# Five more block pairs in seven products, and the SSD output product as filler of attention

## The chip, the cores and the metric

The kernel runs on one core of a Trainium2 chip. The metric is the time of one execution in device microseconds; a kernel is run three times and the median is taken. Besides that, one execution is recorded by the hardware profiler, and all tables of this document come from such records.

## What is computed

One decoder block on 1024 tokens of width 1024, in float32. Two token mixers, a Mamba-2 SSD and a differential attention, run on the same normed input `h`; each is followed by its own output product and a sigmoid gate; the merged result goes through one more product, a residual, and a gated conv-FFN. Cut to what matters here:

```python
h = rms_norm(x, pre_norm1_w) * (1 + sc1) + sh1            # sc, sh, g: six rows of silu(c) @ w_ada + b_ada
z, xbc, dt_raw, q, k, v, gates = split(h @ w_in)
y_ssd = ssd_branch(z, silu(conv(xbc)), dt_raw)            # 8 chunks of 128 tokens, 16 heads in 2 groups
                                                          # ends with * silu(z), RMS over a group, * norm_w
y_att = diff_attention(rope(q), rope(k), v)               # 8 heads, two softmaxes each, 8 query blocks
gate_ssd, gate_att = split(sigmoid(gates))
merged = gate_ssd * (y_ssd @ w_ssd_o) + gate_att * (y_att @ w_attn_o)
x = x + g1 * rms_norm(merged @ w_out, post_norm1_w)
u_gate, u_val = split(conv3(rms_norm(x) @ w_up))
x = x + g2 * rms_norm((gelu(u_gate) * u_val) @ w_down, post_norm2_w)
```

## The kernel before, in words

**Products.** Every float32 product is made of three passes: both operands are split into a high part (`fp32r`, a copy on ScalarE) and a low part (a subtraction on DVE), and TensorE adds high x high, high x low and low x high in one PSUM bank. A *block* is 128 output columns of a weight matrix, over all 1024 tokens. Taken directly it is 2 token halves x 8 k x 3 = 48 matmuls of 128x512. Two blocks can be taken as a *pair*: the 2x2 scheme of Strassen and Winograd, seven products (`order`, L292) of 4 k x 3 matmuls, 84 in all, at the price of sums of weights (`x_sum`, four per pair), sums of `h` made once (`t1` to `t4`), and additions where the banks are emptied.

**Stages, in order of time.** (1) Norm, and the first blocks directly. (2) The *pairs* (loop at L728, list at L293): ten pairs, two of gates of the SSD (`gs`), two `rope` and one `qk` pair (a block of `w_q` with one of `w_k`), five of the SSD's `xbc`. What a pair's result still needs (`post`, L456: tanh and store for gates; RoPE; split and store for q, k; a conv of four taps and SiLU for `xbc`) is worked off during the next pair, step by step, at the products that `steps_at` (L508) names. In the same loop single `ada_sum`s (a dot product of a 128x1024 tile with the condition, on DVE; 32 in all, `ada_load` fetches a tile for each) stand at the products named in `ada_at` (L511). (3) The *z product* (L953): three column thirds of eight token blocks, 24 products `nz`; 20 ada sums; at `nz` 22 `ada_end` (L940): three short DVE operations, a transposition on TensorE, two stores. From `nz` 8 the *down sums* start (`down_sums`, L812): for each of 11 blocks of `w_down`, two loads of 512 KB, four DVE sums of 128x512 and two stores, for the seven products of the down projection. (4) The *SSD chunks* (L1234): 16 units `u` (chunk, group). TensorE's gaps are filled with the v product (`v_stream`, `fill`); three down sums stand in each unit; the normed y of a chunk (`chunk_norm`) is stored to `yd`. (5) A stage of its own (L1307): q block 3, the 64 transpositions of y (`turn_y`, four banks in turn, 16 after another) with the norm weight applied and split, then the SSD output product `so`, eight blocks directly, gated and stored to `msd`. (6) *Attention* (L1623): 64 items (head j, query block i). For each: scores of the next item, transpositions of this item's probabilities, values. The softmax of the next item runs on DVE and ScalarE meanwhile: mask, maximum, two exps, reciprocal, and at L1522 the difference of the two, which the next item's transpositions at L1530 wait for. TensorE's time is filled by `dense_stream` (L1425): 17 blocks, directly: k 3, q and k of 4 to 7, and the eight attention gates `ga`. (7) Attention's output product, `w_out`, and the FFN: the up product in pairs with `up_conv` and `up_gsum` worked off at products (`early`, `convs`), the down product in seven products.

**What sets the order.** TensorE, DVE, ScalarE and SP (in attention GpSimd in SP's place) follow the order of the code within each stage (`manual_schedule`); the planner may interleave the end of one such stage with the start of the next, and it sets the other queues. Every DMA goes through SP's queue but six stores. Work that is to be done "by the way" goes to a list (`later`, `bg`), from which `run_bg(n)` takes the next n pieces; `need(tag)` runs the list until a piece is done. A fill is one k, three matmuls.

In attention an item gets a quota of fills by

```python
share = [5, 4, 4, 4, 5, 5, 5, 4]                                              # by query block i
quota = (j * sum(share) + sum(share[: i + 1])) * nfill // (8 * sum(share)) - done
f1 = quota // 2                       # behind the first transpositions
f2 = (quota - f1 + 1) // 2            # behind the values of the first four key blocks; the rest at the end
```

with `nfill` = 16 per block less `NFIRST` + `NLAST` (L1618).

## Time and profile before

| | |
|---|---|
| three runs | 1846.46, 1847.04, 1847.34 us |
| the profiled execution | 1846.69 us; span from first to last instruction 1844.9 us |
| granted TensorE clock, mean | 0.999 |
| DMA | 327.5 MB, 178 GB/s over the span |
| q 3, turns and `so` (544 to 649 us) | 105 us |

A row of the view by line or by wait gives the line, the engine, the operation, tiles written and read, shapes, the count, the busy time and the mean duration of one; behind the bar the idle time of the engine ahead of these instructions and what ended most of it. A row of the timeline gives start and duration in us from the span's start, and in brackets the idle time before it. Busy time of TensorE includes the overlap of a matmul with the next one, so it is not a measure of how fast matmuls follow each other.

### The profile page before, as it was taken

The numbers are of one execution on the slowest core, as the hardware profiler recorded it, in microseconds if no ns is written. First come the engines' busy times: TensorE is split into PE (matmuls) and PEld (weight loads), VectorE is DVE, ScalarE is ACT, GpSimd is POOL, SyncE is SP. The second block draws the span as 40 slices with busy tenths as digits, with TensorE's granted clock in tenths as the row PEclk, the third lists the DMA queues.
The fourth block names the chain that finished last, engine by engine and source line by source line (L and its number), as shares of the span: only waits on it lengthen the run. The fifth ranks groups of instructions, "written<-read, shape, count | busy, mean of one in ns | idle before, by whom it ended". The sixth has DMA issues, their size and how long they took to land.

```text
span 1844.9 us, 24221 instructions
## 1 busy us (share of the span) xinstructions
PE 1818.2 (99%) x8889; PEld 1518.2 (82%) x8889; DVE 1304.1 (71%) x2000; ACT 877.4 (48%) x1714; POOL 123.5 (7%) x122
## 2 busy tenths in 40 slices
PE   9999999999999999999999999999999999999998
PEld 7788889987788888888887888887878888888886
DVE  7887897778954267677667563588988888876545
ACT  4454453256542145665666232555545454564532
POOL 0000000035630000000000000000000000000001
PEclk9999999999999999999999999999999999999999
DMA  9464546878664746665724663122223222378744
GB/s 373 163 231 157 184 129 220 309 244 301 239 236 140 237 127 172 185 171 156 193 83 165 239 215 141 58 86 109 103 109 112 100 97 109 115 237 306 239 154 158
DMA packets 130726, 327.52 MB, mean 178 GB/s; under 512 B 14208, under 2 KB 38672, under 8 KB 130608
## 3 DMA queue, kind: packets, MB, share of 16 engines
q1 hardware_dynamic: 129648, 322.83, 52.2%
q0 software_dynamic: 960, 3.15, 0.5%
q8 instruction: 70, 1.15, 0.2%
q14 instruction: 48, 0.39, 0.1%
HBM read 228.53 MB, written 95.30 MB: 176 GB/s over the span
## 4 chain that ended last, share of the span: by engine, by line
PE 76%; DVE 12%; ACT 5%; DMA 4%; issue 2%; SPq 0%; POOL 0%; POOLq 0%; DVEq 0%; ACTq 0%
PE upx L1852 3%; PE upx L1851 3%; PE upx L1853 3%; PE o L1543 3%; PE xx L422 2%; PE xx L423 2%; PE xx L424 2%; PE dx L2216 2%; PE dx L2217 2%; PE dx L2215 2%; PE dy L2217 2%; PE dy L2216 2%; PE dy L2215 2%; PE so L119 2%; PE ao L119 2%
## 5 line engine op out<-in xcount | busy, mean ns | idle before, releaser
L1851 PE MATMUL upx<-t,wu_t 128*128 128x512 f32 x264 | 103.3, 391 | 0.3 <-DVE cv L2280 0.2
L1852 PE MATMUL upx<-t,wu_t 128*128 128x512 f32 x264 | 102.9, 390 | 0.2 <-DVE t L1969 0.2
L1853 PE MATMUL upx<-t,wu_t 128*128 128x512 f32 x264 | 102.8, 389 | 0.0
L1825 ACT ACTIVATE wu_t<-sab 128x512 fp32r<-128x512 f32 x57 | 34.1, 627 | 129.7 <-DVE sab L1842 129.7
L1531 ACT COPY aT<-at 128x512 f32<-128x512 f32 (+2 forms) x96 | 46.0, 479 | 94.5 <-PE at L1530 94.5
L1543 PEld LDWEIGHTS o<-vt,aT 128*128 128x128 f32 x576 | 74.8, 191 | 10.3 <-ACT aT L1531 6.3
L96 DVE TENSOR_TENSOR g_lo<-gst,g_hi 128x1024 fp32r<-128x1024 f32 (+1 forms) x42 | 47.5, 1135 | 50.6 <-ACT g_hi L95 50.6
L1543 PE MATMUL o<-vt,aT 128*128 128x128 f32 x576 | 81.2, 277 | 0.6 <-ACT aT L1531 0.3
L95 ACT ACTIVATE g_hi<-gst 128x1024 fp32r<-128x1024 f32 (+1 forms) x42 | 41.4, 988 | 64.8 <-DMA gst<-gld_s 34.8
L1504 DVE TENSOR_REDUCE nmx<-sc 128x1 f32<-128x640 f32 (+3 forms) x64 | 65.6, 1025 | 2.2
L1484 PE MATMUL sc<-kst,qst 128*128 128x512 f32 (+2 forms) x192 | 64.0, 341 | 0.1
L1485 PE MATMUL sc<-klo,qst 128*128 128x512 f32 (+2 forms) x192 | 63.1, 345 | 0.0
L1869 DVE SCALAR_TENSOR_TENSOR ug<-cg,vec,ug 128x1023 f32<-128x1023 f32 (+1 forms) x44 | 56.3, 1281 | 7.7 <-ACT ug L1868 6.9
L1851 PEld LDWEIGHTS upx<-t,wu_t 128*128 128x128 f32 x264 | 49.6, 188 | 11.9 <-DVE cv L2280 1.6
L1852 PEld LDWEIGHTS upx<-t,wu_t 128*128 128x128 f32 x264 | 49.6, 188 | 10.6 <-DVE t L1969 0.5
L1829 DVE TENSOR_TENSOR wu_t<-sab,wu_t 128x512 fp32r<-128x512 f32 x57 | 39.4, 690 | 26.5 <-ACT wu_t L1825 26.5
L1853 PEld LDWEIGHTS upx<-t,wu_t 128*128 128x128 f32 x264 | 49.6, 188 | 10.3
L1520 DVE RECIPROCAL rsm<-ssum 128x2 f32<-128x2 f32 x64 | 10.6, 166 | 65.7 <-ACT p L1517 36.9
L1869 DVE SCALAR_TENSOR_TENSOR uv<-cv,vec,uv 128x1023 f32<-128x1023 f32 (+1 forms) x44 | 56.3, 1279 | 0.9 <-ACT uv L1868 0.9
L1522 DVE SCALAR_TENSOR_TENSOR p<-p,coef,p 128x128 f32<-128x128 f32 (+3 forms) x64 | 52.4, 819 | 2.3
L1530 PE MATMUL at<-ident,p 128*128 128x128 f32 x288 | 48.0, 275 | 4.2 <-DVE p L1522 4.1
L2216 PE MATMUL dx<-wdt_lo,g_hi 128*128 128x512 f32 x132 | 51.4, 389 | 0.0
(567 smaller groups left out, 5828.6 us busy)
## 6 DMA issues: line engine op xcount, KB each, us to landing
adas<-in_w_ada SPq DMA_DIRECT2D x32, 512.0 KB, 4.7
wdr<-in_w_down SPq DMA_DIRECT2D x22, 512.0 KB, 5.3
wtd<-wdr SPq DMA_DIRECT2D x22, 512.0 KB, 2.9
wuf<-in_w_up SPq DMA_DIRECT2D x22, 512.0 KB, 3.4
gld_s<-gsum SPq DMA_DIRECT2D x22, 512.0 KB, 2.8
gst<-gld_s SPq DMA_DIRECT2D x20, 512.0 KB, 4.3
wdt_raw<-wtd SPq DMA_DIRECT2D x20, 512.0 KB, 5.1
wuv<-in_w_up SPq DMA_DIRECT2D x19, 512.0 KB, 3.5
```

The source lines that it names most:

```text
L119: T.matmul(ps, ll, rh, start=False, stop=(i == n - 1))
L1484: T.matmul(sc[:, n0:n1], qs_[s][:, tsl], ks_[s][:, n0:n1], start=True, stop=False)
L1485: T.matmul(sc[:, n0:n1], qs_[s][:, tsl], kl[s][:, n0:n1], start=False, stop=True)
L1504: V.reduce_max(nmx[:, bq, s : s + 1], sc[:, :L], axis=AX.X, negate=True)
L1543: T.matmul(po_of[j, grp][:, qi, :], at[:, k, :], vt[j % 2][:, kt, :], start=(kt == 0), stop=(kt == i))
L1851: T.matmul(out_, wh, xh_, start=(k == 0 and first), stop=False, skip_group_check=not first)
L1852: T.matmul(out_, wh, xl_, start=False, stop=False, skip_group_check=not first)
L1853: T.matmul(out_, wl, xh_, start=False, stop=(k == end), skip_group_check=not first)
L1869: V.scalar_tensor_tensor(u[:, d:], c_[:, : S - d], fw[:, 2 - d : 3 - d], u[:, d:], op0=ALU.mult, op1=ALU.add)
L2215: T.matmul(o, gh[:, kk, tsl], wh, start=(k == 0 and not more), stop=False, skip_group_check=more)
L2216: T.matmul(o, gh[:, kk, tsl], wl, start=False, stop=False, skip_group_check=more)
L2217: T.matmul(o, gl[:, kk, tsl], wh, start=False, stop=(k == KF - 1), skip_group_check=more)
```

## The change

1. Five pairs are added to the list of the pairs: four of gates (blocks 8 to 15, which are the attention gates) and q, k block 3. The `xbc` pairs come last, as before, now as numbers 10 to 14. The tanh of the attention gates and their store to `gad` happen in `post`.
2. 22 ada sums move into pairs 6 to 10, so that all 32 are done there; `ada_end` moves to z product 2. The conv steps of the first `xbc` pair stand one product later in pair 0.
3. The down sums start in pair 11: four steps in each of the last four pairs, 28 in z, none among the SSD chunks.
4. y keeps its own three tiles; the norm weight is applied with the scale (a row broadcast, `nwr`); from unit 3 each unit ends with the turn of one (chunk, group): four transpositions in the bank `wb` that `py` also uses, high part by ScalarE, low part by DVE, one store to `ytd`. The last three turns stand at the start of attention.
5. The stage of its own is gone. Attention's dense stream has 16 blocks: q, k of 4 to 7, then the eight blocks of `so`. Its right operand, the turned y, is loaded from `ytd` into freed tiles of `h` while blocks 6 and 7 run; gating (`gated`, DVE) and the store to `msd` come from the list of background work.
6. Seven in place of four pieces of attention's result are split behind the last item; `NFIRST` is 12.
7. In the FFN Gelu stands at step 3 of `up_conv` in place of step 2, and in `early` the steps of block 6 come one product later.

```diff
-    pairs = [("gs", 4, 5), ("rope", 0, 0), ("gs", 6, 7), ("rope", 1, 1), ("qk", 2, 2)] + [("xbc", b, b + 1) for b in range(2, 12, 2)]
+    pairs = [("gs", 4, 5), ("rope", 0, 0), ("gs", 6, 7), ("rope", 1, 1), ("gs", 8, 9), ("qk", 2, 2), ("gs", 10, 11)]
+    pairs += [("qk", 3, 3), ("gs", 12, 13), ("gs", 14, 15)] + [("xbc", b, b + 1) for b in range(2, 12, 2)]
...
-                SP.dma_start(gsd[b], c_)
+                SP.dma_start((gsd + gad)[b], c_)
...
-    ada_at = {0: (6,), 1: (0, 1, 2, 3, 5, 6)} | {m: (6,) for m in range(5, 10)}
+    ada_at = {0: (6,), 10: (0, 1, 2)} | {m: (0, 1, 2, 3, 5, 6) for m in (1, 7, 9)} | {m: (1, 2, 3, 5, 6) for m in (6, 8)}
+    conv_at = ({1: (0,), 2: (1,), 3: (4,), 4: (2, 5), 5: (6,), 6: (3, 7)}, steps_at["xbc"])
...
+                if (m, p) in ((10, 3), (10, 5), (11, 0), (11, 1)):
+                    down_load(*divmod(((10, 3), (10, 5), (11, 0), (11, 1)).index((m, p)), 2))
+                if m > 10 and p in (2, 3, 4, 6):
+                    next(sums_dn)
...
-                if nz == 22:
+                if nz == 2:
                     ada_end()
...
+                for _ in range(2 if nz in (8, 10, 12, 14) else 1):
                     next(sums_dn)
...
-                V.tensor_scalar(y[:, gs], y[:, gs], ssy[:, c, g : g + 1], 0.5, op0=ALU.mult, op1=ALU.mult)
-            SP.dma_start(yd[c], y)
+                V.scalar_tensor_tensor(y[:, gs], y[:, gs], ssy[:, c, g : g + 1], nwr[:, gs], op0=ALU.mult, op1=ALU.mult)
...
+    def turn_y(c, g):
+        ps = ps_wb(f"ytr{c}_{g}")
+        for q in range(4):
+            T.transpose(ps[:, q * P : (q + 1) * P], yt[c % 3][:, (4 * g + q) * P : (4 * g + q + 1) * P], ident)
+        st = yst[g]
+        p4 = ps.rearrange("p (k t) -> p k t", t=P)
+        s4 = st.rearrange("p (k n) t -> p k n t", n=2)
+        A.activation(s4[:, :, 0, :], p4, AF.Copy)
+        V.tensor_tensor(s4[:, :, 1, :], p4, s4[:, :, 0, :].bitcast(F32), op=ALU.subtract)
+        SP.dma_start(ytd[:, 8 * g : 8 * g + 8, c * P : (c + 1) * P], st.bitcast(F32))
+    blocks = [(kind, b) for b in range(4, 8) for kind in ("w_q", "w_k")] + [("w_ssd_o", j) for j in range(8)]
...
             chunk_state(u)
             fill(1 if u % 3 else 0)
             run_bg(1)
             if u % 2 == 1:
                 chunk_norm(u // 2)
+            if u >= 3:
+                turn_y(*divmod(u - 3, 2))
...
+    def load_yT(k, half):
+        SL.put(hT[k][half])
+        yT[k][half] = new_hl(f"yT{k}_{half}")
+        SP.dma_start(yT[k][half].bitcast(F32), ytd[:, 2 * k : 2 * k + 2, half * HALF : (half + 1) * HALF])
+    def gated(j, half, ps):
+        def f_():
+            hsl = slice(half * HALF, (half + 1) * HALF)
+            V.scalar_tensor_tensor(mouts[j % 2][:, hsl], gths[j % 2][:, hsl], 1.0, ps, op0=ALU.add, op1=ALU.mult)
+            if half == 1:
+                SP.dma_start(msd[j], mouts[j % 2])
+                load_gate(j + 2)
+        bg.appendleft((("gated", j, half), f_))
...
-    NFIRST, NLAST = 8, 20
+    NFIRST, NLAST = 12, 20
...
-        for _ in range(NFIRST - 6):
+        turn_y(6, 1)
+        for n in range(NFIRST - 6):
             fill(1)
             run_bg(2)
+            if n == 3:
+                turn_y(7, 0)
+                turn_y(7, 1)
...
-            if step == 2:
+            if step == 3:
                 A.activation(g_, g_, AF.Gelu_apprx_tanh)
...
-        early += [[(up_gsum, 5, 0), (up_gsum, 5, 1)], [(up_gsum, 5, 2), (up_conv, 6, 0)], [(up_gsum, 5, 3), (up_conv, 6, 1)]]
-        early += [[(up_conv, 6, i)] for i in range(2, 5)] + [[]]
+        early += [[(up_gsum, 5, 0), (up_gsum, 5, 1)], [(up_gsum, 5, 2)], [(up_gsum, 5, 3), (up_conv, 6, 0)]]
+        early += [[(up_conv, 6, i)] for i in range(1, 5)]
```

More of the change, by code (lines that the diff above doesn't have):

```diff
@@ L937 @@
     dec = None
-    adas = [SL.get(f"adas{i}") for i in range(3)]
     def ada_end():
@@ L1022 @@
     assert n_ada == 32
-    SL.put(*ev, *adas, crow, zraw)
+    assert next(sums_dn, None) is None
+    SL.put(*ev, zraw, *wdr[0], *wdr[1])
     singles.close()
```

343 lines of the change are left out of this document (133 added, 210 removed).

## Prediction, made before the changed kernel ran

> **What bounds the kernel now.** I read the head of the page first, then the busy time by stage, then the list of who waited on TensorE, then the order of time around each place that the diff touches.
>
> ```profile
> span 1844.9 us, 24221 instructions
> ...
> PE 1818.2 (99%) x8889; PEld 1518.2 (82%) x8889; DVE 1304.1 (71%) x2000; ACT 877.4 (48%) x1714; POOL 123.5 (7%) x122
> ```
> ```profile
> 92.50:284.00 191.50, 190.89 (x841) 157.41 (x841) 160.86 (x217) 94.90 (x145) 0.00 (x0) 1.00 0.54 182
> 284.00:380.00 96.00, 94.79 (x601) 93.96 (x600) 67.10 (x129) 24.76 (x46) 0.00 (x0) 1.00 0.78 268
> 380.00:544.00 164.00, 160.68 (x831) 127.12 (x830) 126.84 (x185) 92.44 (x246) 82.73 (x63) 1.00 0.73 253
> 649.00:1022.00 373.00, 367.60 (x2131) 312.55 (x2130) 257.43 (x531) 220.93 (x591) 16.11 (x16) 1.00 0.55 158
> ```
> The columns are the stretch, its length, busy PE, PEld, DVE, ACT and POOL, the granted clock, the DMA share and GB/s. The stretches are the ten pairs, the z product, the SSD chunks with the v product as filler, and attention with its dense filler. TensorE is busy all but some 27 us of the span, so the time is the number of matmuls times their pitch, plus the few places where TensorE waits. A matmul's duration overlaps the next one; the pitch is what counts:
>
> ```profile
> 90.28 0.39 PE L119 MATMUL gs<-hT,wgs_lo 128*128 128x512 f32 x1
> 90.51 0.39 PE L117 MATMUL gs<-hT,wgs_hi 128*128 128x512 f32 x1
> ```
> 0.23 us from start to start (0.227 over a pair: 191.5 us / 10 / 84 = 0.228). The waits of TensorE that the change can touch:
>
> ```profile
> PE at L1530 <- DVE p L1522: 4.1, 10, 0.9
> PE upy L1851 <- ACT evs L2277: 1.9, 2, 1.6
> PE pst L1168 <- DVE tt L1151: 1.5, 2, 0.9
> ...
> PE v L1073 <- DVE wv_lo L930: 0.8, 1, 0.8
> PE po L1150 <- DVE prev L1170: 0.7, 1, 0.7
> ...
> PE adat L946 <- DVE gcol L944: 0.6, 1, 0.6
> PE xx L422 <- ACT xevs L750: 0.5, 1, 0.5
> ```
> (total us, times, longest.)
>
> **The change part by part.** The sum is made against the profiled execution: 1846.69 us, its span of 1844.9 and 1.8 around it; the median of the three runs is 0.35 higher.
>
> *Fewer matmuls, -13.6.* Two blocks taken directly are 2 x 48 = 96 matmuls of 128x512; as a pair they are 7 products x 4 k x 3 = 84. Five new pairs save 60 x 0.227 = 13.6 us. All five sit in the stage where TensorE already runs at its pitch. The SSD output product (384 matmuls) only moves. The 64 turns of y stay 64.
>
> *More DVE work in the pairs, +0.5.* 22 of the 32 ada sums come to pairs 6 to 10, and 16 of the 44 down sums to the last four.
>
> ```profile
> 112.40:131.40 19.00, 19.00 (x85) 15.73 (x85) 16.17 (x27) 9.20 (x16) 0.00 (x0) 1.00 0.78 280
> 245.90:265.00 19.10, 19.10 (x86) 15.83 (x85) 17.19 (x23) 10.65 (x16) 0.00 (x0) 1.00 0.35 111
> ```
> ```profile
> L398 DVE TENSOR_TENSOR xw_t<-xsab,xw_t 128x512 fp32r<-128x512 f32 x30 | 20.7, 691 | 14.0 <-ACT xw_t L397 14.0
> L185 DVE CUSTOM_DVE_ANT_0 adas<-adas,crow,vec 128x1024 f32<-128x1024 f32 x12 | 15.4, 1280 | 2.4 <-DMA adas<-in_w_ada 2.4
> ...
> L499 DVE SCALAR_TENSOR_TENSOR xbcT<-xcv,vec,xbcT 128x1023 f32<-128x1023 f32 x5 | 6.4, 1283 | 0.0
> ...
> L406 DVE TENSOR_TENSOR xsab<-xwf,xsab 128x512 f32<-128x512 f32 x9 | 6.2, 688 | 0.0
> ```
> The first stretch is pair 1, which carries six ada sums already: DVE 16.17 of 19.0, DMA 0.78, TensorE without a gap. Pairs 6 to 9 become like it (two of them with q, k: two splits of 1.2 us more), and SP's order there (a sum frees a tile, a load follows, the next weights queue behind it) is also that of pair 1. A pair with conv behind it is the second stretch: 17.19 busy with one ada sum. The last four lose that sum (1.3) and get four down sums (4 x 0.69, some 2.5 where they follow each other): about 18.4 of 19.05. DVE in order also waits there for ScalarE's high halves (14.0 us over 30 splits), so it will run late; the splits stand three products (3 x 12 x 0.227 = 8.2 us) ahead, and z has room. Ends: 0, and 4 us if each pair is late by 1. I take 0.5, near the row of pair 1. The two w_down loads and two stores per block go through SP in the same stretch at a DMA share that was 0.35.
>
> *The first conv taps of pair 0 one product later, -0.5.* That is the wait for xevs above, 0 to -0.7.
>
> *z: the gates' end moves from product 22 to product 2, +2.3.* `ada_end` issues three short DVE operations and then a transposition on TensorE, ahead of z product 3.
>
> ```profile
> 291.98 0.18 DVE L976 TENSOR_TENSOR sm<-z,rows 128x16 f32<-128x16 f32 x1 [0.70 <-PE z L119]
> ...
> 293.09 1.28 DVE L499 SCALAR_TENSOR_TENSOR xbcT<-xcg,vec,xbcT 128x1022 f32<-128x1022 f32 x1
> ...
> 375.42 0.28 PE L946 MATMUL adat<-ident,gcol 128*16 128x128 f32 x1 [0.56 <-DVE gcol L944]
> ```
> At product 22 it cost 0.6. At product 1 now, DVE starts behind the product at 291.98 (bias), waits for ScalarE, scales, and ends the conv tap at 294.37: 2.4 us. Product 2 will have the same queue ahead of the gate operations (3 x 0.16): TensorE stands for about 2.9, and nothing else is in its order there. 2.9 - 0.6 = 2.3; ends 1 and 4. Behind the waiting transposition stands all of z. The granted clock is 1.00 in every stage above. The Trainium skill, "TensorE: Matmul & The Clock Gate", section "Why this matters for your kernels", asks for no idle gap over about 3 us on TensorE, else its clock falls to half; by the row the sum gets 2.3 here, by that page also what rival 4 costs, should the gap come out longer. No run here shows a gap of that length. The 20 ada sums that leave z (1.28 each) outweigh the 20 more down sums (0.69), and their 20 loads of 512 KB make room for seven blocks' w_down traffic.
>
> *SSD without down sums, -3.0.*
>
> ```profile
> L814 DVE TENSOR_TENSOR wdr<-wdr 128x512 f32<-128x512 f32 x9 | 10.4, 1153 | 0.0
> ```
> The waits for tt, prev and wv_lo (1.5 + 0.7 + 0.8) are DVE held up by w_down: it waits in order for a load, and its sums take longer in this stage, where GpSimd works (1.15 us against the 0.69 of the same shape in the pairs). What comes in is lighter: per unit one copy on ScalarE and one subtraction on DVE, some 0.6 and 0.7 us, and 4 transpositions; their bank is `py`'s, whose reader ends within 1 us while TensorE has three fills (2 us) to go. Ends -4 and 0.
>
> *The seam from SSD to attention, +5.5.* Now w_q block 3 follows the last v without a gap, its split made long before. After the change the last turns of y stand there, two by two in one bank, and the first split of w_q 4 is behind one of them in the order.
>
> ```profile
> 544.13 0.39 PE L117 MATMUL w_qp<-hT,w_q_hi 128*128 128x512 f32 x1
> 544.33 0.59 ACT L1089 COPY vev<-v 128x512 f32<-128x512 f32 x1 [5.69 <-PE v L1074]
> ...
> 549.58 1.91 PE L1293 MATMUL ytr<-ident,yr 128*128 128x128 f32 x16
> 550.21 2.42 ACT L1295 ACTIVATE yT<-ytr,vec 128x512 fp32r<-128x512 f32 x4 [3.20 <-PE ytr L1293]
> 550.93 2.73 DVE L1296 SCALAR_TENSOR_TENSOR yT<-ytr,vec,yT 128x512 fp32r<-128x512 f32 x4 [2.01 <-ACT yT L1295]
> ```
> Turn to turn in one bank: from 549.58 to the DVE's end (550.93 + 0.69 + 0.1) is 2.1, of which 0.45 is work: 1.7 idle, once before turn (6,1) and once before (7,1). Behind (6,1): copy 0.6, high half 0.6, low half 0.7 and three hand-overs, less the two matmuls that need the high half alone: 2.0 idle. Sum 5.4. Ends 2 (the planner finds other work between) and 8 (the last chunk's norm, which shares ACT and DVE, comes ahead).
>
> *Attention with one block less, +6.8 given back.* The loop's fills go from 244 to 224 (17 blocks x 16 - 28 to 16 x 16 - 32); a fill is 3 matmuls, 0.68 us. By the quota formula item 0 loses one in all eight heads, items 2 and 4 one in four heads, item 6 two in four and one in four, items 1 and 7 gain one in four. What an item's fills cover is the next item's softmax:
>
> ```profile
> 789.98 0.48 DVE L1522 SCALAR_TENSOR_TENSOR p<-p,coef,p 128x256 f32<-128x256 f32 x1
> ...
> 790.90 0.27 PE L1530 MATMUL at<-ident,p 128*128 128x128 f32 x1
> ```
> ```profile
> 750.80 0.62 DVE L1522 SCALAR_TENSOR_TENSOR p<-p,coef,p 128x384 f32<-128x384 f32 x1
> ...
> 751.57 0.30 PE L1530 MATMUL at<-ident,p 128*128 128x128 f32 x1 [0.94 <-DVE p L1522]
> ```
> ```profile
> 779.37 1.28 DVE L1522 SCALAR_TENSOR_TENSOR p<-p,coef,p 128x1024 f32<-128x1024 f32 x1
> ...
> 781.58 0.29 PE L1530 MATMUL at<-ident,p 128*128 128x128 f32 x1
> ```
> ```profile
> 823.25 1.28 DVE L1522 SCALAR_TENSOR_TENSOR p<-p,coef,p 128x1024 f32<-128x1024 f32 x1
> ...
> 824.77 0.41 PE L1530 MATMUL at<-ident,p 128*128 128x128 f32 x2
> ```
> Where TensorE waits (751.57) it starts 0.15 after DVE's end, so the slack is the distance less 0.15: 0.29 behind item 0, 0.78 and 0.09 behind item 6 of an even and an odd head. Losses: item 0, 8 x (0.68 - 0.29) = 3.1; item 6, 4 x (1.36 - 0.78) + 4 x (0.68 - 0.09) = 4.7; item 2, taken like item 0, 4 x 0.39 = 1.6; item 4 none. Item 1's extra fill covers waits like that of 751.57: ten are 4.1 us, so 4 x 0.41 = 1.6 back. Sum 7.8. ScalarE loses 16 tanh of the gates, which stood among the exps, DVE gets 16 gated products: I take off 1.0. Ends 1.5 and 13.6 (every lost fill turns into waiting).
>
> *Gelu a step later, -1.9.* The wait for evs above is a ScalarE copy behind a Gelu that waits for DVE; at the later step its input is long done. Ends -2.3 and 0.
>
> Sum: -13.6 + 0.5 - 0.5 + 2.3 - 3.0 + 5.5 + 6.8 - 1.9 = -3.9, so 1842.8 by the profiled execution; I forecast **1842.8 us**.
>
> **The rivals.**
> 1. *Covers hold*: attention gives back 1.5, the seam costs 2. For it: ScalarE is freed of tanh, and the planner already puts the split of w_q 3 among SSD work. Against: the slacks above. 1842.8 - 5.3 - 3.5 = 1834.0.
> 2. *Attention returns everything*: all 20 fills turn into waits, 6.8 more: 1849.6. For it: ten items already wait. Against: slack up to 0.78.
> 3. *The other side: DVE bounds the last four pairs.* Its operations are 14 x 0.69 + 6 x 1.28 + 4 x 0.69 = 20.1 us by duration, and 1.9 of 19.1 are idle today; if neither overlaps, 22.0 against 19.05, 2.95 late a pair, 11.8 over four: 1842.8 - 0.5 + 11.8 = 1854.1. It decides once DVE needs over 19.05 a pair and the lead of 8.2 is gone. Against: pair 8's operations add up to 18.7 but show 17.19 busy, since they overlap.
> 4. *A cold clock*: if TensorE ran at half rate for one z product (3.8 us) behind each of the two long idle stretches, 7.6 more, 1850.4. Against: the clock is 1.00 in every stage above, those with waits among them. (The Trainium skill's page on the clock gate, named at z, is what speaks for it.)
>
> **How the numbers follow.** A measurement of this kernel tells 0.2% (3.7 us) from no change: faster is below 1843.3, slower above 1850.7. My forecast 0.45, with its own range 1838 to 1847, half of it faster; rival 1 0.24; rival 2 0.14 (a third of it slower); rival 3 0.13; rival 4 0.04. Faster 0.23 + 0.24 = 0.47, slower 0.13 + 0.05 + 0.02 = 0.20, same 0.33. The range 1833 to 1851 takes in all but rival 3 and the tails of 1 and 2.
>
> **What would show it.** Right: pairs of 19.05 us also in the last four; a transposition `adat` in early z with 2 to 3 us idle before it; no waits for tt, prev, wv_lo; two waits of `ytr` and one of `w_qp` at the seam; waits for p of 10 to 13 us in place of 4.1; no wait for evs. Wrong: attention not shorter than 365 us, or idle time before the pairs' matmuls, or a granted clock under 0.95 behind a gap.

## The result, and the profile after

The changed kernel takes **1853.60 us** (median of six, 1853.01 to 1855.37) against 1847.19 of the kernel before on the same chip (median of six): a ratio of 1.0036, 95% interval 1.0023 to 1.0049. It is slower by 6.4 us where 3.9 us less was forecast, and the time lies above the range. The profiled execution took 1854.85 us with a span of 1853.1, 8.2 over the span of before.

The head of the page, and the changed kernel's waits of TensorE (total us, times, longest):

```profile
span 1853.1 us, 24191 instructions
...
PE 1814.6 (98%) x8829; PEld 1510.9 (82%) x8829; DVE 1326.0 (72%) x2059; ACT 896.2 (48%) x1749; POOL 118.2 (6%) x122
```
```profile
PE w_ssd_op L1374 <- DMA yT<-ytd: 3.8, 1, 3.8
PE at L1468 <- DVE p L1460: 3.5, 8, 0.9
PE ytr L1207 <- DVE yst L1212: 3.0, 2, 1.6
PE adat L952 <- DVE gcol L950: 2.7, 1, 2.7
...
PE z L117 <- ACT xcv L837: 1.9, 1, 1.9
PE xx L423 <- DVE xcv L794: 1.5, 3, 0.9
...
PE sc L1423 <- DMA klo<-kld: 1.2, 1, 1.2
PE w_qp L1374 <- ACT w_q_hi L1238: 1.2, 1, 1.2
PE px L1112 <- ACT M L1134: 1.2, 1, 1.2
```
8889 matmuls have become 8829, the 60 that were to go. The waits for `tt`, `prev`, `wv_lo` and `evs` are gone. But TensorE's busy time fell by only 3.6 us, not by 13.6: part of the remaining work ran slower. The same execution by stage (fifteen pairs, z, SSD, attention, the rest), each from its first matmul to the next one's; behind the engines' columns stand the granted clock, the DMA share and GB/s:

```profile
94.26:384.52 290.26, 286.94 (x1261) 236.05 (x1260) 241.93 (x346) 135.31 (x211) 0.00 (x0) 1.00 0.64 222
384.52:482.48 97.96, 95.25 (x597) 94.81 (x597) 55.48 (x109) 25.12 (x45) 0.00 (x0) 0.98 0.79 266
482.48:653.70 171.22, 167.40 (x892) 134.01 (x890) 104.82 (x163) 100.74 (x262) 77.72 (x63) 1.00 0.47 147
653.70:1032.60 378.90, 366.40 (x2088) 306.12 (x2089) 266.33 (x550) 215.72 (x582) 16.85 (x17) 0.98 0.66 192
1032.60:1853.08 820.48, 811.65 (x3605) 670.32 (x3603) 582.05 (x763) 376.17 (x576) 21.41 (x36) 1.00 0.43 150
```
and, of the kernel before, z up to its last matmul, 0.15 us short of the first v product:

```profile
284.19:379.18 94.99, 93.78 (x597) 93.09 (x596) 66.91 (x129) 24.22 (x43) 0.00 (x0) 1.00 0.78 267
```
Two stages of after show a clock of 0.98; before, none did. The clock's record lists its slow stretches, in which half of the clock was granted (*half clock* from here on): at 14.56 us (6.83 long), 400.27 (3.41), 652.86 (6.83), 878.13 (6.83) and the last 4 us; before has only one, in the last 5 us, when TensorE is done. The matmul rows show what that costs. Behind the transposition `adat`:

```profile
395.86 0.32 PE L119 MATMUL z<-wz_hi,hT 128*128 128x346 f32 x1
398.88 0.28 PE L952 MATMUL adat<-ident,gcol 128*16 128x128 f32 x1 [2.71 <-DVE gcol L950]
...
400.12 0.37 PE L118 MATMUL z<-wz_lo,hT 128*128 128x346 f32 x1
400.29 0.49 PE L119 MATMUL z<-wz_hi,hT 128*128 128x346 f32 x1
400.58 0.49 PE L117 MATMUL z<-wz_hi,hT 128*128 128x346 f32 x1
```
The pitch (start to start) goes from 0.16 to 0.29 us, 1.4 us *behind* the gap, and back after 3.41 us. The seam and the wait for yT:

```profile
649.77 0.60 PE L1207 MATMUL ytr<-ident,yt 128*128 128x128 f32 x4
651.84 0.66 PE L1207 MATMUL ytr<-ident,yt 128*128 128x128 f32 x4 [1.47 <-DVE yst L1212]
653.70 0.79 PE L1374 MATMUL w_qp<-hT,w_q_hi 128*128 128x512 f32 x1 [1.21 <-ACT w_q_hi L1238]
654.29 0.63 PE L1375 MATMUL w_qp<-hT,w_q_hi 128*128 128x512 f32 x1
```
```profile
877.00 0.30 PE L1423 MATMUL sc<-klo,qst 128*128 128x128 f32 x1 [1.23 <-DMA klo<-kld]
...
881.60 0.80 PE L1374 MATMUL w_ssd_op<-yT,w_ssd_o_hi 128*128 128x512 f32 x1 [3.84 <-DMA yT<-ytd]
```
At both places the matmuls behind the waits run at half rate. Why yT is late stands in the rows of SP's queue:

```profile
851.98 1.53 SPq L1342 DMA_DIRECT2D yT<-ytd  x2
...
867.09 1.49 SPq L1246 DMA_DIRECT2D klo<-kld  x2
869.03 8.22 SPq L1401 DMA_DIRECT2D vt<-vd  x8
877.30 2.91 SPq L1342 DMA_DIRECT2D yT<-ytd  x4
```
Four of the eight loads of half 1 are issued at 877.30, behind the next head's q, k and V; TensorE wanted them at 877.76.

My theory after this reading: three things weigh, the yT loads that I had priced at nothing (about 7 us with what follows them), half clock behind the stalls (about 6 us) and a second bank that VectorE empties too late in the last four pairs (about 3 us). Sixteen kernels test that, and two more the version that came out of it. Every ratio is to the kernel before, run beside it on the same chip.

### The profile page after: what moved, and what is told of

The parts are those of the page before. It is cut to its first block, busy times and chain, and to the rows that moved or that the text cites. A ratio compares the mean times of both kernels' runs of the same rounds, so it can differ in the third digit from the quotient of the medians.

```text
span 1853.1 us, 24191 instructions
## 1 busy us (share of the span) xinstructions
PE 1814.6 (98%) x8829; PEld 1510.9 (82%) x8829; DVE 1326.0 (72%) x2059; ACT 896.2 (48%) x1749; POOL 118.2 (6%) x122
## 4 chain that ended last, share of the span: by engine, by line
PE 80%; DVE 8%; DMA 5%; ACT 4%; issue 2%; SPq 1%; POOL 0%; POOLq 0%; DVEq 0%; ACTq 0%
PE upx L1797 4%; PE upx L1798 4%; PE upx L1796 4%; PE o L1481 3%; PE xx L423 2%; PE xx L425 2%; PE xx L424 2%; PE upy L1798 2%; PE upy L1796 2%; PE upy L1797 2%; PE dx L2161 2%; PE dx L2162 2%; PE dx L2160 2%; PE z L117 2%; PE z L118 2%
## 5 line engine op out<-in xcount | busy, mean ns | idle before, releaser
L398 ACT ACTIVATE xw_t<-xsab 128x512 fp32r<-128x512 f32 x45 | 27.3, 627 | 93.3 <-DVE xsab L407 93.2
L423 PE MATMUL xx<-xt,xw_t 128*128 128x512 f32 x180 | 70.5, 392 | 1.5 <-DVE xcv L794 1.5
L425 PE MATMUL xx<-xt,xw_t 128*128 128x512 f32 x180 | 70.1, 389 | 0.0
L424 PE MATMUL xx<-xt,xw_t 128*128 128x512 f32 x180 | 70.0, 389 | 0.0
L1374 PE MATMUL w_ssd_op<-yT,w_ssd_o_hi 128*128 128x512 f32 x128 | 57.8, 452 | 3.8 <-DMA yT<-ytd 3.8
L1796 PEld LDWEIGHTS upx<-t,wu_t 128*128 128x128 f32 x264 | 49.5, 188 | 11.6 <-DVE cv L2225 1.3
L1797 PEld LDWEIGHTS upx<-t,wu_t 128*128 128x128 f32 x264 | 49.6, 188 | 10.7 <-DVE t L1914 0.5
```

Of the source, the lines that this page charges most:

```text
L423: T.matmul(o, wh, xh_, start=(k == 0 and first), stop=False, skip_group_check=not first)
L424: T.matmul(o, wh, xl_, start=False, stop=False, skip_group_check=not first)
L425: T.matmul(o, wl, xh_, start=False, stop=(k == KH - 1), skip_group_check=not first)
L1374: T.matmul(ps, w[0][:, k, :], xh_, start=(k == 0), stop=False)
L1796: T.matmul(out_, wh, xh_, start=(k == 0 and first), stop=False, skip_group_check=not first)
L1797: T.matmul(out_, wh, xl_, start=False, stop=False, skip_group_check=not first)
```

## Experiments: the yT loads

```diff
-                r = 8 * (i - 14) + k if i < 16 else 8 * (i - 16) + k
-                if 14 <= i < 18 and r % 2 == 1:
-                    load_yT(r // 2, i // 16)
+                if i in (14, 16):
+                    load_yT(k, i // 16)
```


> The eight yT loads of a half are issued together at unit 14 (half 0) and unit 16 (half 1) instead of one for every two steps over two units each; nothing else. Theory (the last loads come late because they stand on SP's queue behind the next head's loads): the wait of w_ssd_op on yT (3.8 us) and the slow products behind it (1.7 us) go, about 5.5 us in all, 1848 us. If the wait of sc on klo (1.2 us) goes too, 6.7 us. Rival (the DMA engines are full there, and what comes earlier only pushes another transfer back): the wait moves to klo, qst or vt with 3 us or more, and the gain is below 2 us.

1854.99 us, ratio 1.0043 (1.0029 to 1.0057): no gain. The wait for yT is gone, another has its place:

```profile
PE sc L1421 <- DMA vt<-vd: 4.1, 1, 4.1
...
PE sc L1422 <- DMA klo<-kld: 1.8, 2, 1.0
```
The rival holds for this order, one load at each of a unit's eight steps: eight loads ahead of the head's loads make the head late (its V is issued at 872.18 us in place of 869.03). It does not yet say whether the bytes are too many or only badly placed.

Then the loads taken away:

```diff
-        SL.put(hT[k][half])
-        yT[k][half] = new_hl(f"yT{k}_{half}")
-        SP.dma_start(yT[k][half].bitcast(F32), ytd[:, 2 * k : 2 * k + 2, half * HALF : (half + 1) * HALF])
+        yT[k][half] = hT[k][half]
```

> The sixteen loads of yT are left out; the SSD output product reads the q, k operands that are still there, so its values are another computation, with the same matmuls. Theory (the loads fill the DMA engines around 840 to 885 us, and whatever comes last on SP's queue there is waited for): no wait for yT, klo or vt is left, 5 us of waits and up to 3.4 us of half clock go, attention from its first w_qp to ao takes 371 to 373 us instead of 378.9, and the time is 6 to 8 us below the changed kernel, about 1847 us. Rival (the waits there are an order of SP's queue, and the head loads would come late all the same): a wait of 2 us or more for klo, kst or vt stays, and the gain is below 4 us.

1847.77 us, ratio 0.9998 (0.9989 to 1.0007). From the first `w_qp` to `ao` 371.8 us instead of 378.9, and no wait for a DMA in attention:

```profile
652.67:1024.47 371.80, 363.29 (x2089) 304.20 (x2089) 266.31 (x550) 215.79 (x582) 16.83 (x17) 1.00 0.61 173
```
So the loads cost 7.1 us, more than the whole loss of 6.4. Then spread:

```diff
-                r = 8 * (i - 14) + k if i < 16 else 8 * (i - 16) + k
-                if 14 <= i < 18 and r % 2 == 1:
-                    load_yT(r // 2, i // 16)
+                for hf in range(2):
+                    r = 8 * (i - 13 - 2 * hf) + k
+                    if 0 <= r < 24 and r % 3 == 2:
+                        load_yT(r // 3, hf)
```


> The yT loads of a half are spread over three units instead of two (half 0 over units 13 to 15, half 1 over 15 to 17; a load for each third step, starting in the unit that last reads the slots). Theory (the DMA engines are full only because 4 MB are asked for in 27 us; over 40 us they fit): the wait for yT falls from 3.8 us to below 1, that for klo below 1, no half clock there, 5 to 7 us less than the changed kernel, about 1848 us. Rival (the same bytes push the head's loads back wherever they lie): another wait for vt, kst or klo of 2 us or more, gain below 3 us.

1850.97 us (six runs, 1848.67 to 1857.69), ratio 1.0021 (1.0005 to 1.0036). In the profile attention takes 372.7 us, with a wait for yT of 1.2 and none for klo:

```profile
652.75:1025.49 372.74, 363.97 (x2089) 304.20 (x2089) 266.38 (x550) 215.74 (x582) 16.82 (x17) 1.00 0.67 195
```
There nearly all of the 7.1 comes back with the same bytes, so it was their place, not their number. But this execution is the fastest of the six. By the ratios the gain is 2.8 us, where leaving the loads out gains 7.0 and 5 to 7 were forecast: three units are a better place, and not yet a safe one.

## Experiments: the last four pairs

The down sums out of the pairs and into z:

```diff
-                if m > 10 and p in (2, 3, 4, 6):
-                    next(sums_dn)
...
-                for _ in range(2 if nz in (8, 10, 12, 14) else 1):
+                for _ in range(2 if nz < 20 else 1):
```


> No down sums in the last four pairs; all 44 of them are taken during the z products (two for each of the first twenty z steps and one after that). Theory (the bank of the second product has to be emptied by VectorE within one product, and the down sums stand ahead of that copy on VectorE): the waits of xx on the copy xcv (1.5 us, three times) and the gap of 2.2 us at the start of z go, the pairs take 286.5 to 287.5 us instead of 290.2, and the time is 3 us below the changed kernel, about 1850.5 us. Rival 1 (the four pairs are bound by their splits, not by the sums): the pairs stay at 290 and the time stays within 1 us of the changed kernel. Rival 2 (VectorE then bounds the z products): pairs as in the theory, but z longer by 3 us or more, and no gain in all.

1862.28 us, ratio 1.0080 (1.0065 to 1.0095). The pairs take 286.7 us, as the theory has it. z and the SSD behind it pay for that twice:

```profile
379.71:482.67 102.96, 95.43 (x589) 94.17 (x590) 65.11 (x123) 23.94 (x43) 0.00 (x0) 0.98 0.85 296
482.67:660.32 177.65, 170.01 (x899) 136.33 (x896) 105.95 (x164) 101.44 (x263) 76.25 (x63) 0.98 0.47 148
```
These stretches go from z's first matmul to the first `px`, and from there to `w_qp`; in the changed kernel they take 97.3 and 171.9. Both are 5.7 us longer. VectorE is busy for only 65 of 103 us in the first, so the second rival is right in its outcome, and not by VectorE's busy time. TensorE waits 2.2 us for `wz_hi`, 2.3 for `wz_lo` and 5.0 for `wv_lo`. VectorE, in order, stands 7.3 us ahead of its sums until their loads land, and ahead of `wv_lo` 6.0 us for a copy of ScalarE. That the traffic of the sums (a DMA share of 0.85) holds back the weights is argued, not shown. That the sums sit in the pairs pays.

The same sums at other products of the same pairs:

```diff
-                if m > 10 and p in (2, 3, 4, 6):
+                if m > 10 and p in (0, 1, 5, 6):
```


> The same sixteen down sums in the last four pairs, but at products 0, 1, 5 and 6 instead of 2, 3, 4 and 6: no sum is ahead of the copy xcv of the second bank any more within two products, and nothing is added to the z products. Theory (VectorE is late only at that place; over a pair it has room, 17.3 us of 19.05): the waits of xx on xcv go and the pairs take 287 to 288 us instead of 290.2, 1.5 to 3 us gained, about 1851 us. Rival (a pair with four sums is full on VectorE wherever they stand): the wait moves to another bank or to the splits, and the pairs stay within 0.5 us of 290.

1855.39 us, ratio 1.0038 (1.0025 to 1.0051). The pairs take 289.3 us; the three waits on `xcv` (1.5 us) are two (0.8), the wait at the start of z 1.5 instead of 1.9. A part of the theory only: one microsecond, between both forecasts, and too little for the total to show.

## Experiments: the gates' end in z, and the clock

```diff
+                if nz == 2:
+                    ada_end()
                 if nz < 8:
                     post(last_pair, nz)
-                if nz == 2:
-                    ada_end()
```


> The end of the gates (ada_end) is issued ahead of the conv step that now stands before it at z step 2, nothing else. Both theories: the gap ahead of the transposition adat shrinks from 3.0 us to about 1.7 us, which is worth 1.3 us. Theory (the eleven z products at 0.288 us behind it instead of 0.160 are the answer of the clock to the length of the gap): with the shorter gap the granted clock stays at 1.00 in the 8 us behind it and another 1.4 us is gained, 2.7 us in all, about 1851 us. Rival (the slow products come from somewhere else, whatever the gap): the clock there stays near 0.57 over 4 us, and the gain is 1.3 us at most.

1853.42 us, ratio 1.0032 (1.0019 to 1.0045). adat's wait is 1.5 us, and behind it the clock stays at 1.00. z to the first v product takes 96.75 us instead of 97.96; the total does not tell it from the changed kernel's. But this execution shows half clock from 385.06 on, behind the 2.3 us wait at the start of z, where the changed kernel's profile with 1.9 shows none. And of the eleven profiles with the wait of 2.7 us at adat, four show half clock behind *it* and seven none. A gap's length alone does not decide. I therefore laid a grid of 3.413 us through the record's slow stretches (in the changed kernel they start 113, 74 and 66 such steps after each other) and took TensorE's busy share in each of its windows. In the changed kernel, from the grid:

```profile
383.20:386.62 3.42, 2.10 (x13) 2.10 (x14) 2.11 (x3) 1.94 (x3) 0.00 (x0) 1.00 1.08 412
396.86:400.27 3.41, 1.39 (x9) 1.39 (x10) 2.80 (x7) 0.01 (x1) 0.00 (x0) 1.00 0.97 327
649.45:652.86 3.41, 1.58 (x11) 0.97 (x9) 1.77 (x2) 1.41 (x3) 0.53 (x1) 1.00 0.34 115
659.69:663.10 3.41, 1.86 (x11) 1.44 (x10) 0.69 (x1) 0.60 (x1) 0.00 (x0) 1.00 0.99 277
874.72:878.13 3.41, 1.81 (x12) 1.33 (x10) 1.91 (x3) 0.40 (x2) 0.00 (x0) 1.00 0.44 118
```
and the one long gap of the kernel before (a wait of 1.6 us in the FFN):

```profile
1351.99:1355.40 3.41, 1.80 (x9) 1.17 (x8) 3.02 (x4) 2.44 (x4) 0.00 (x0) 1.00 0.62 220
```
The first number behind the length is TensorE's busy time. Behind 1.39 and 1.58 of 3.41 the next window runs at half clock, behind 1.86 and 2.10 not; 1.80 and 1.81 went either way. Over all twenty traces of this study, between 25 and 1830 us: of the windows that ran at full clock, all 32 with a busy share up to 0.45 were followed by half clock, 6 of the 31 from 0.46 to 0.57, and 1 of the 127 from 0.58 to 0.80. The same gap costs in one execution and not in the next, as the grid cuts it.

The gates' end back where it was:

```diff
-                if nz == 2:
+                if nz == 22:
                     ada_end()
```


> The end of the gates back at z step 22, where it stood in the kernel before; all else as in the changed kernel. Theory: the wait of adat falls from 2.7 us to 0.6, and z (from its first product to the first v product) takes 95.1 us where 97.3 and, without the half clock, 95.7 were seen: 94 to 95 us. Rival (at step 22 something else has to wait for the gates by now): a new wait of 1 us or more at the end of z or the start of the SSD, z at 96 us or more.

1851.21 us, ratio 1.0022 (1.0012 to 1.0032), some 2.4 below the changed kernel (the intervals of the two ratios overlap). adat waits 0.6 us, z to the first v product takes 95.98 us instead of 97.96, and up to 1.7 of the 95.98 is half clock at z's start (3.41 us from 384.12). Without the half clock it is inside the forecast. Two waits change places with it: that of `px` for M (1.2) is gone, and that of v for `wv_lo` (0.7) is back.

## Experiments: the seam

```diff
-        turn_y(6, 1)
         for n in range(NFIRST - 6):
             fill(1)
             run_bg(2)
-            if n == 3:
+            if n == 1:
+                turn_y(6, 1, ps_wc)
+            if n == 5:
                 turn_y(7, 0)
-                turn_y(7, 1)
+                turn_y(7, 1, ps_wc)
```


> The last three turns of y stand among the first products of attention's projections instead of ahead of them (chunk 6, second half, behind the second fill; chunk 7 behind the sixth), two of them in the other bank; nothing is left out. Theory (waits of 1.6, 1.4 and 1.8 us with half clock behind them): the waits lie beside the fills, and 4.7 us of gaps and about 3.0 us of slow products go, 7.7 us in all, about 1846 us. Rival 1 (the fills then wait for w_q's split, which ended late behind the work of the SSD): a wait of 2 us or more at the first w_qp stays, and the gain is 3 to 5 us. Rival 2 (only the gaps matter, the clock is low there for another reason): clock of 0.5 over 654 to 659 stays, and the gain is 4.7 us at most.

1856.14 us, ratio 1.0043 (1.0028 to 1.0058). From the first `px` of the SSD to the first `w_qp` it is 3.6 us faster; to the first `w_kp`, 23 us behind that, nothing is left of it (191.4 us from `px` to `w_kp`, 191.0 in the changed kernel):

```profile
PE sc L1423 <- DMA klo<-kld: 3.3, 2, 1.7
...
PE sc L1422 <- DMA kst<-khd: 2.7, 1, 2.7
```
```profile
651.20 0.58 SPq L1243 DMA_DIRECT2D qst<-qd  x1
651.82 1.80 SPq L1246 DMA_DIRECT2D kst<-khd  x2
653.67 1.24 SPq L1246 DMA_DIRECT2D klo<-kld  x2
```
Neither theory nor rivals had this: the first scores need head 0's second loads, which are issued 2.7 to 5.1 us after the last product of v (648.52) and land only after 659 us. The seam's waits lay partly *under* that. Is it the traffic of y's stores that delays them? The same seam without any DMA of y, neither its stores (below) nor its loads (as above):

```diff
-        SP.dma_start(ytd[:, 8 * g : 8 * g + 8, c * P : (c + 1) * P], st.bitcast(F32))
```


> The seam with the turns among the first fills, but y neither stored nor loaded (the output product reads the q, k operands, as in the run without the loads). Theory (the 8 MB of y's stores and head 0's loads fill the DMA engines at the seam, so that what the turns no longer cost is waited for at kst and klo): without the stores these waits fall below 1 us, and the time is 4 to 7 us below the run that leaves out the loads alone, about 1842 us. Rival (head 0's second loads come late because their slots come free only at the end of the SSD): waits for kst and klo of 2 us or more in all stay at the first scores, gain below 3 us.

1848.50 us, ratio 1.0006 (0.9997 to 1.0015), no better than the 1847.77 without the loads alone; kst and klo are still waited for at the first scores, 1.8 and 1.7 us (2.7 and 1.6 with y's DMA). The rival: y's traffic is not the main cause. That the slots come free too late is read from the code (they are put back behind the last chunk and taken at once); no run gave them other slots.

The stalls left where they are, and TensorE kept busy in them by matmuls that nobody reads:

```diff
+        keep_busy(5)
         turn_y(6, 1)
+        keep_busy(4)
...
                 turn_y(7, 0)
+                keep_busy(5)
                 turn_y(7, 1)
```


> Fourteen matmuls of 128x512 whose result nobody reads, in the three places at the seam where TensorE stands (5 ahead of turn (6,1), 4 behind it, 5 ahead of turn (7,1)); no wait is taken away. Theory (the clock is halved by the share of a window of 3.41 us in which TensorE was busy, not by the wait): no half clock between 645 and 665 us where every run of this order of the seam has shown 3.4 or 6.8 us of it, and a time 1.5 to 3.5 us below the changed kernel. Rival (the half clock has another cause, such as the load on the DMA engines there): it stays, and the time is the same or longer by the matmuls that don't fit into the gaps.

```profile
649.26 1.41 PE L1565 MATMUL busy<-hT 128*128 128x512 f32 x5
650.98 0.66 PE L1207 MATMUL ytr<-ident,yt 128*128 128x128 f32 x4 [0.30 <-DVE yst L1212]
651.39 1.17 PE L1565 MATMUL busy<-hT 128*128 128x512 f32 x4
652.84 0.50 PE L1374 MATMUL w_qp<-hT,w_q_hi 128*128 128x512 f32 x1 [0.28 <-ACT w_q_hi L1238]
```
The clock stays at 1.00 from 645 to 665 us, with the DMA engines as full as before (a share of 0.99 from 653 to 657 us in both). One execution alone would prove little: of the twelve profiles with this order of the seam and without these matmuls two show no half clock there either (the sums in z, the four moves below). But ten do, and none of the four profiles with the matmuls: the half clock follows TensorE's idleness. The time does not follow: 1855.18 us, ratio 1.0044 (1.0030 to 1.0058). From `w_qp` to `w_kp` it takes 18.0 instead of 19.1 us, and attention as a whole 379.7: the wait for yT stands (3.7), with 10.24 us of half clock around it in this execution.

## Experiments: the fills of a head, and the FFN

The 28 fills of a head dealt out otherwise:

```diff
-    share = [5, 4, 4, 4, 5, 5, 5, 4]
+    share = [10, 7, 7, 6, 6, 6, 8, 6]
```


> The 28 fills of a head are dealt out as 5, 3, 4, 3, 3, 3, 4, 3 over its eight items instead of 3 to 4 each in the proportion 5, 4, 4, 4, 5, 5, 5, 4; their number stays. Theory (what attention gave back is softmax that a shorter item no longer covers, and items 3 to 5 have 0.9 to 1.3 us to spare): the waits of the transposition on p fall from 3.5 us (eight) to below 1 us, and the time by 2 to 3 us, about 1851 us. Rival (the sums of start to start rose for other reasons, so the eight waits are replaced by waits of other items): the waits for p stay at 3 us or more, gain below 1 us.

1859.81 us, ratio 1.0061 (1.0046 to 1.0076). Worse by 6, and the rival in kind: the waits for p became twelve with 4.0 us in place of eight with 3.5, and a split of `w_k`, which is taken from the background list item by item, came late (2.3 us, with half clock behind it).

Two kernels for the two edits in the FFN, the Gelu back at step 2, and the list `early` of before with the Gelu left at step 3:

```diff
-            if step == 3:
+            if step == 2:
                 A.activation(g_, g_, AF.Gelu_apprx_tanh)
```


> The Gelu back at step 2; all else as in the changed kernel. Theory: the wait of upy on evs (1.9 us, two times in the kernel before) comes back, and the time from the first upx to the first dx is 1.5 to 2.5 us longer than the 424.1 us of the changed kernel. Rival (that stretch got shorter for another reason): no wait for evs, and 424 us as before.

```diff
-        early += [[(up_gsum, 5, 0), (up_gsum, 5, 1)], [(up_gsum, 5, 2)], [(up_gsum, 5, 3), (up_conv, 6, 0)]]
-        early += [[(up_conv, 6, i)] for i in range(1, 5)]
+        early += [[(up_gsum, 5, 0), (up_gsum, 5, 1)], [(up_gsum, 5, 2), (up_conv, 6, 0)], [(up_gsum, 5, 3), (up_conv, 6, 1)]]
+        early += [[(up_conv, 6, i)] for i in range(2, 5)] + [[]]
```


> The list of early steps of the FFN as it stood in the kernel before; the Gelu stays at step 3; all else as in the changed kernel. Theory (the wait for evs was made by that list, since the Gelu back at step 2 did not bring it back): a wait of upy on evs of about 1.6 us comes back, and the time from the first upx to the first dx is 425.5 to 427 us instead of 424.1. Rival (the wait needs both, or was made elsewhere): no wait for evs, 424 to 424.5 us.

From the first `upx` to the first `dx` the kernel before takes 426.7 us and the changed one 424.1. With the Gelu back it is 424.5 and no wait for evs: the rival. With the old list it is 425.9, and a wait of 1.4 us is back near the same place, for `cv` instead of evs. (1856.22 us, ratio 1.0049, and 1856.86 us, 1.0051; two runs each, too few to tell them from the changed kernel.) The list makes most of what I had put down to the Gelu.

## Experiments: what is left when the causes are taken away

Four moves together: yT over three units, sums at products 0, 1, 5 and 6, `ada_end` at step 22, and z's first loads earlier in the last pair, whose diff is the only new one:

```diff
-                    z_raw += [fetch_z(*thirds[0], kp) for kp in {1: (0,), 2: (1,), 3: (2, 3)}.get(p, ())]
+                    z_raw += [fetch_z(*thirds[0], kp) for kp in {0: (0, 1, 2), 3: (3,)}.get(p, ())]
```


> Four moves together, nothing left out: the yT loads over three units (as measured alone), the down sums at products 0, 1, 5 and 6 (as measured alone), the first three wz_raw loads at product 0 of the last pair instead of at 1, 2 and 3, and the end of the gates back at z step 22. Theory (each stall has a cause of its own and they add up): attention 372.7 us instead of 378.9 (-6.2), the pairs -1.0 and the start of z another -1.5 (its wait for the copy xcv was ScalarE behind splits that waited for late loads), adat's wait 2.7 to about 0.5 (-2.2) with no half clock there (-1.7 in the runs where it fell): 11 to 12.5 us below the changed kernel, about 1842 us, 0.3% under the kernel before. Rival (what is removed in one place is waited for in the next, as with the sums in z and the share of fills): less than 8 us of it are kept, 1846 us or more.

1846.26 us (eleven runs), ratio 0.9992 (0.9983 to 1.0001). 7.3 us below the changed kernel where 11 to 12.5 were forecast: attention 373.9 (the forecast 372.7), pairs 288.9, z 94.4. By the total that is the rival's range. By stage the moves do add up; attention kept a wait for yT of 1.7 us and klo one of 0.9. I had also added up half clock that not every execution has.

On top of it the moved turns, with more fills ahead:

```diff
-    NFIRST, NLAST = 12, 20
+    NFIRST, NLAST = 18, 20
```


> The four moves, and the last three turns of y among the first fills, with eighteen fills instead of twelve ahead of attention's loop (twelve of them ahead of the first scores), which leaves 218 instead of 224 for the loop. Theory (the seam's waits can be covered if the first scores come behind the landing of head 0's second loads, some 10 us after the end of the SSD): 4.7 us of waits and 1.7 us of half clock at the seam go, no wait for kst or klo of over 1 us takes their place, and six fills less in the loop cost up to 3: 3 us below the four moves alone. Rival (the loop pays in full, or the loads land later still): no gain, or up to 2 us worse.

1847.59 us, ratio 1.0004 (0.9995 to 1.0012): the rival. The first scores no longer wait over 1 us, but the six fills are missed in the loop: waits for p 7.1 us over sixteen items instead of 4.2 over nine, and the dense stream, six fills ahead, meets yT too early again (4.2).

And on the four moves, instead of that, the fourteen matmuls that kept the seam busy:

> The four moves together with the fourteen matmuls at the seam. Theory: the half clock that most of the runs of the four moves still show by their mean clock (0.995 to 0.999) goes, 0 to 2 us less than the four moves, about 1845 us, just below the kernel before. Rival: the matmuls come later than the data they stand in front of, and the time is 1 us above the four moves.

1845.54 us (eleven runs), ratio 0.9992 (0.9983 to 1.0001), no difference that the intervals tell from the four moves. The wait for yT was 3.3 us in this profile. So the last question was again yT. In place of the three units:

```diff
-                for hf in range(2):
-                    r = 8 * (i - 13 - 2 * hf) + k
-                    if 0 <= r < 24 and r % 3 == 2:
-                        load_yT(r // 3, hf)
+                r = 8 * (i - 13) + k if i < 15 else 8 * (i - 15) + k
+                if 13 <= i < 15 and r % 2 == 1:
+                    load_yT(r // 2, 0)
+                if 15 <= i < 18 and r < 20 and r % 5 in (2, 4):
+                    load_yT(2 * (r // 5) + (r % 5 == 4), 1)
```


> As the four moves with the seam kept busy, but the yT loads of half 0 over units 13 and 14 (every second step) and those of half 1 over the twenty steps from unit 15 on, so that the last is asked for four steps (2.7 us of fills, some 6 us of time) earlier. Theory (what is left of the yT wait, 3.3 us with half clock behind it, is a last load asked for too late): the wait falls below 1 us, no half clock there, 2 to 4 us less than with three units each, about 1842.5 us, 0.25% under the kernel before. Rival (the DMA engines are full there whatever the order, and the head's loads come late instead): a wait for vt, kst or klo of 2 us or more, no gain.

and with half 1 closer together:

```diff
-                if 15 <= i < 18 and r < 20 and r % 5 in (2, 4):
-                    load_yT(2 * (r // 5) + (r % 5 == 4), 1)
+                if 15 <= i < 18 and r < 16 and r % 2 == 1:
+                    load_yT(r // 2, 1)
```


> As the one with twenty steps, but half 1 over the sixteen steps of units 15 and 16: the spacing of the changed kernel, one unit earlier. Theory (lateness of the last load): no wait for yT, and the same time as with twenty steps, about 1842.5 us. Rival (the rate of the loads is what fills the DMA engines): waits for klo, kst or vt of 2 us or more around 860 us, 2 us or more above the one with twenty steps.

1843.11 us (ten runs), ratio 0.9976 (0.9967 to 0.9986), and **1842.49 us** (six runs), ratio 0.9969 (0.9957 to 0.9981). With twenty steps 1.4 us of the wait for yT are left, where less than 1 was expected; with sixteen none, and one for klo of 1.5 us. SP's queue shows why:

```profile
842.66 0.94 SPq L1342 DMA_DIRECT2D yT<-ytd  x2
...
844.67 1.76 SPq L1342 DMA_DIRECT2D yT<-ytd  x2
...
859.35 1.34 SPq L1246 DMA_DIRECT2D klo<-kld  x2
861.33 9.14 SPq L1403 DMA_DIRECT2D vt<-vd  x8
```
The last yT load is issued ahead of the next head's loads. The faster rate was not worse, so it was the place in the queue. Both beat the kernel before, and the changed one by 10.5 to 11 us.

## Why the prediction was wrong, by its own steps

- **Fewer matmuls, -13.6: right.** 60 are gone, at a pitch of 0.227 outside the slow stretches.
- **DVE in the pairs, +0.5, and the conv taps, -0.5: too small.** By the pace of before (191.64 us for ten) fifteen pairs take 287.5; they took 290.3, 2.8 more with the wait at z's start, though the wait for xevs is gone. The failed step is "the splits stand three products ahead (8.2 us)": that lead belongs to the splits. The bank of the second product has to be emptied within one product of 2.7 us, and VectorE came to it late (three waits on `xcv`, 1.5 us). Moving the sums gave back 1.0, taking them out of the pairs 3.5. Rival 3's place, at a quarter of its price; that its 1854.1 lies beside the measured 1853.6 is chance.
- **Gates' end, +2.3: right** (0.6 became 2.7), but for the half clock behind it.
- **SSD, -3.0: right for tt and prev.** A wait of 1.2 us for M is new, so 1.8 is left. And `wv_lo` (0.8) was not held up by down sums among the SSD chunks: in the six profiles with the gates' end back at step 22 that wait is there again (0.7 to 0.8) without any, and the one for M is gone.
- **Seam, +5.5: near** in its waits (3.0 for ytr and 1.2 for w_qp), without the half clock. The idea that covering it would pay in full was wrong too: head 0's second loads stand behind it.
- **Attention, +6.8: too large for the fills, and a cost left out.** The waits for p, forecast at 10 to 13 us, were 3.5, against 4.1 before: the lost fills did not turn into waits. From start to start, scores to transposition took 14.8 us before and 16.5 after (63 times), fill to transposition 9.5 and 10.5, fill to values 15.3 and 16.5, fill to `ot` 4.3 and 3.8: 3.4 in all, nearer to rival 1's 1.5, and no run shows what made them. What failed most is the step that never costs the sixteen yT loads. The moved product brought sixteen DMAs of 512 KB onto SP's queue among the heads' loads, and the sum has no line for them: 7.1 us by the run without them. This term alone is larger than the loss.
- **Gelu, -1.9: near in size by luck** (426.7 to 424.1), wrong in cause: by the two runs mostly the list.
- **Rival 4, the cold clock, had 0.04.** The argument against it, a clock of 1.00 in stages with waits among them, was an argument from a kernel whose gaps were short or cut by the grid. 17.1 us of the changed kernel behind 25 us ran at half clock; TensorE was busy in 12.8 of them, so some 6.4 us of work are lost, by estimate. The Trainium skill, "TensorE: Matmul & The Clock Gate", section "What's actually happening", speaks of a free-running window of 3413 ns; the traces agree with that length. The Trainium skill's rule on the same page, section "Why this matters for your kernels", of no gap over some 3 us was too lenient here: a stall of 1.5 us and the first 0.4 of the next, in one window of the seam, were enough.

Of the signs named beforehand, adat's wait, two waits of ytr and one of w_qp came, and those for tt, prev, wv_lo and evs went; the longer waits for p and the unhindered last pairs did not come. All three signs of being wrong came as well: attention of 378.9 us, not under 365; idle time ahead of `xx`; half clock behind a gap.

Against the forecast's -3.9 the span's +8.2 is 12.1 us more. By estimate it is made of: yT and klo 5.0, half clock 6.4, the pairs 2.8, the wait for M 1.2 and 1.7 of a later first pair, less 3.4 in attention, 0.7 in the FFN, 1.3 at the seam and 0.2 at the gates' end. That is 11.5; the other 0.6 stays unplaced. The later first pair is not the change's: of the twenty profiles the seven with half clock between 14 and 23 us began it at 93.6 to 94.4 us (the changed kernel's among them), the thirteen without at 92.2 to 93.2.

## What to carry to other kernels

When a product is moved into another stage, price its operands' loads there first: on which queue, behind which loads, and when each is due; by the profiles the same sixteen loads cost 7.1 us in one place and 0.9 spread over three units. A bank's lead is counted from the product that needs it next, not from the splits. On a kernel whose TensorE is 99% busy, add to every stall what the clock does behind it, and look at stalls together when they lie within a few microseconds.

## What the hardware showed unexpectedly

In these twenty traces the granted clock changes on a fixed grid of 3.41 us, at another phase in each execution, and by TensorE's share of busy time: up to 0.45 always half clock in the next window (32 times), from 0.58 on almost never (1 of 127). It comes after the gap and lasts 3.41, 6.83 or (twice) 10.24 us; z's matmuls in it follow each other at 0.29 us instead of 0.16. With fourteen matmuls of no use at the seam none of four profiles showed it there, without them ten of twelve, while DMA ran at a share of 1.0.
